# Attention values from weight tiles of 512 rows by 512 columns

## The chip, the cores and the metric

The kernel runs on one core of a Trainium2 chip. What counts is the device time of one execution in microseconds. Five engines work side by side: TensorE (PE in the profile, its weight loads PEld) multiplies matrices and writes to PSUM, VectorE (DVE), ScalarE (ACT) and GpSimd (POOL) do the rest, and SyncE (SP) issues most of the DMAs.

## What is computed

The reference runs 256 tokens of 1024 features through two layers of a first block and then through a second block. The change touches the values of two attentions. In layer 0 of the first block the mixer is a differential attention of four heads beside a pooling branch:

```python
def even_mixer(h, w_in, w_out, ...):
    proj = h @ w_in
    q = proj[..., :A_QK_COLS].reshape(B, S, A_HEADS, 2, A_QK_DIM)
    k = proj[..., A_QK_COLS:2 * A_QK_COLS].reshape(B, S, A_HEADS, 2, A_QK_DIM)
    v = proj[..., 2 * A_QK_COLS:2 * A_QK_COLS + A_WIDTH].reshape(B, S, A_HEADS, A_V_DIM)
...
    o = diff_attention(q[..., 0, :], q[..., 1, :], k[..., 0, :], k[..., 1, :], v, lam, bias_dist)
```

In both layers a cross-attention reads a memory of 256 tokens, the same for both layers:

```python
def cross_attention(h, mem_n, wq, wkv, wo):
    q = (h @ wq).reshape(B, S, X_HEADS, X_HEAD_DIM)
    kv = (mem_n @ wkv).reshape(B, M, 2, X_HEADS, X_HEAD_DIM)
    s = jnp.einsum('bshd,bmhd->bhsm', q, kv[:, :, 0]).astype(jnp.float32) * X_HEAD_DIM ** -0.5
    p = jax.nn.softmax(s, axis=-1)
    o = jnp.einsum('bhsm,bmhd->bshd', p.astype(h.dtype), kv[:, :, 1]).reshape(B, S, D_MODEL)
    return o @ wo
```

The first attention has 512 columns of values (`A_WIDTH`), the memory 1024 in each layer.

## The kernel before

Activations stand with features on partitions. Every operand of a large product is the sum of two float32r parts, `hi` and `lo`; a product is three matmuls, hi by hi, hi by lo and lo by hi. Weights come as tiles of 1 MB, cut on the host (`TILES`, `_tiles`), in one fixed order (`plan`, `self.order`). A tile is loaded by SP into one of four staging buffers (`dma_next`), then split in two halves (`prep_next`): ScalarE casts a half to `hi` (line 319), VectorE subtracts it from the float32 weights to give `lo` (line 198). The two parts lie in a ring of four buffers each, so a tile's first cast waits until TensorE has read the tile four places before it for the last time. `take` hands out the next tile, `pump` keeps three ready.

`pair` makes two blocks of 128 output features from one tile: weights are the stationary operand and 256 tokens stream. For values the tokens have to be on partitions, so `natural` turns this round: blocks of 128 tokens are stationary, the weights stream, 256 columns at a time. A tile of 1024 rows by 256 columns gives 2 blocks of tokens by 8 blocks of rows by 3 matmuls, which is 48. Its result is one bank of PSUM, taken from three that rotate (`gbank`). Scores, turned weights and outputs use four others (`abank`).

The orders of TensorE and of SP are those of the program text. ScalarE, VectorE and POOL are put in order by the framework's planner when the kernel is built: at each engine the first ready instruction by its estimate, those of higher priority first; `high_priority(-later)` lowers the priority of weight casts, of the memory's operand and of some pooling work. A buffer that is named by tag comes free when all that reads it is done; until then the next writer waits.

In the first attention (`layer0_mixer`) the keys, queries and the pooling's inputs come first, then scores of heads 0 and 1, then: values 0, turn of head 0 (`diff_T`), scores 2, output 0 (`diff_out`), turn 1, values 1, output 1, scores 3, then the keys of the memory (`mem_k`). `diff_T` transposes a head's weights on TensorE, and ScalarE copies them to `pt` (line 639), a buffer of tag `sq`. There are two of these, and POOL's window sums (`pool_step`, tiles `pwt`) use them too. `vals` evacuates values to `dv`, part of `dvu`, on ScalarE.

In the cross-attention (`cross`) four value tiles are made by `mem_v`, and the rest of the work is hung between them by the table `after`. `turn` is `x_T`: four transposes and a split of the result into two tiles `xpt`, both of tag `sq`. `out` is `x_out`: 12 matmuls of the values `vh` and `vl` with `xpt`, then a split into the operand of the output product.

Of the kernel before, what the change touches and what calls it, by code (L numbers as in the profile page):

```python
# [30 lines left out]
# columns of the table of parameter vectors, 128 values to a column  # L31
# [9 lines left out]
for _n, _k in VCOLS:  # L41
# [5 lines left out]
# matrices of weights, cut into tiles of k blocks of 128 rows by n columns  # L47
TILES = {
    "ab_w_in": (8, 256), "ab_w_out": (8, 256), "conv_w_in": (8, 256), "conv_w_out": (8, 256),
    "xattn_wq": (8, 256), "xattn_wkv": (8, 256), "xattn_wo": (8, 256), "mlp_w1": (8, 256),  # L50
# [5 lines left out]
def _tiles(a, k, n):  # L56
    """[layers, rows, columns] to [layers, row tile, column tile, partition, k * n]"""
    l, r, c = a.shape
    a = a.reshape(l, r // (k * P), k, P, c // n, n).transpose(0, 1, 4, 3, 2, 5)
    return np.ascontiguousarray(a).reshape(l, r // (k * P), c // n, P, k * n)  # L60


def _layout(inputs):
    """weights by tiles, activations and parameter vectors with features on partitions"""
    out = {}
    for name, (k, n) in TILES.items():
        a = np.asarray(inputs[name])
# [5 lines left out]
    # the modulation's weights with output features on partitions  # L73
# [66 lines left out]
class Operand:  # L140
    """an activation, features on partitions, as the sum of two float32r parts"""
# [16 lines left out]
class Kernel:  # L158
# [53 lines left out]
    def w(self, key, name, l, c0, ncol):  # L212
        """256 columns at a time of a matrix of 1024 rows"""
        for c in range(c0 // T, (c0 + ncol) // T):
            self.order.append((key, self.a[name][l, 0, c], 256, 8))

    def plan(self):
# [4 lines left out]
        w("u", "ab_w_in", 0, 1536, 512), w("v", "ab_w_in", 0, 1024, 512)  # L222
        w("xk", "xattn_wkv", 0, 0, D)
# [9 lines left out]
        w("xk", "xattn_wkv", 1, 0, D)  # L233
# [15 lines left out]
    def plan_ada(self, start, j, span, n=12):  # L249
        """n loads of the modulation's weights among the items from start"""  # L250
# [9 lines left out]
    X_ORDER = tuple((key, i) for key in ("xq", "xv") for i in range(4))  # L260

    def plan_x(self, l):
        for key, h in self.X_ORDER:
            if key == "xq":
                self.w("xq", "xattn_wq", l, T * h, T)
            else:
                self.w("xv", "xattn_wkv", l, D + T * h, T)
        self.w("xo", "xattn_wo", l, 0, D)
# [16 lines left out]
    def dma_next(self, part=None, parts=4):  # L285
        """the next weights from DRAM, all of them or a part"""
# [131 lines left out]
    def norm_mean(self, acc, parts=False):  # L418
        """mean of squares over D, on every partition: PSUM [P, T]"""
# [11 lines left out]
    def rsqrt(self, out, m, scratch, scale=1.0, gain=1.0, eps=EPS):  # L431
        """out = gain * (scale * m + eps) ** -0.5: a guess by exp and ln, and one Newton step"""
# [31 lines left out]
    def norm_columns(self):  # L464
        """1 / 16 of the norm's scale as columns by token: [P, 2]"""
# [7 lines left out]
    def r_columns(self, r, c=None):  # L473
        """r [P, T], the same on every partition, as columns by token: [P, 2]"""
# [11 lines left out]
    def pair(self, key, x, ko=False, bank=None, start=True, stop=True, k0=0, k1=8, w=None,  # L486
             mid=None):
        """two blocks of 128 output features: [P, 2, T]"""
# [12 lines left out]
    def halves(self, key, x, k0):  # L501
        """four pairs: the blocks of x from k0 for all of them first, then the others"""
# [10 lines left out]
    def natural(self, key, x, w=None):  # L513
        """[token, 2, 256 output features] with tokens on partitions"""
        wh, wl = w or self.take(key)
        v = self.gbank().rearrange("p (t n) -> p t n", t=2)
        for t in range(2):
            s = slice(t * P, (t + 1) * P)
            for k in range(8):
                self.mm(v[:, t, :], x.hi(k, s), wh[:, k, :], t == 0 and k == 0, False)  # L520
                self.mm(v[:, t, :], x.lo(k, s), wh[:, k, :], False, False)
                self.mm(v[:, t, :], x.hi(k, s), wl[:, k, :], False, t == 1 and k == 7)
        return v
# [5 lines left out]
    def residual(self, i, v, col, last_norm=None):  # L529
        """h += v for pair i, then the next module's operands"""  # L530
# [36 lines left out]
    def diff_setup(self):  # L567
        """the bias by distance, then its band for every query row; lambda"""
# [110 lines left out]
    def pool_windows(self):  # L679
        """means over windows, less the token itself"""  # L680
# [7 lines left out]
    def pool_step(self, i):  # L688
        """the windows of pair i of the groups"""
# [51 lines left out]
    def layer0_mixer(self):  # L741
# [46 lines left out]
        def vals(i):  # L788
            v = self.natural("v", x)
            for t in range(2):  # L790
                self.actf(self.dv[:, t, 256 * i:256 * i + 256], v[:, t, :], AF.Copy,
                          scale=rc[:, t:t + 1])
            self.pump()

        pts = {}
        vals(0)
        pts[0] = self.diff_T(e.pop(0))
        e[2] = self.diff_scores(2)
        self.diff_out(0, pts.pop(0))
        pts[1] = self.diff_T(e.pop(1))  # L800
        vals(1)
        self.diff_out(1, pts.pop(1))
        e[3] = self.diff_scores(3)
# [38 lines left out]
    def mem_v(self, i, vx):  # L842
        v = self.natural("xv", self.mem)
        self.split(*(a[:, :, 256 * i:256 * i + 256] for a in vx), v)
        self.pump()
# [42 lines left out]
    def cross(self, l):  # L888
# [16 lines left out]
        def out(h):  # L905
# [3 lines left out]
                 ("xv", 1): [(out, 0), (turn, 1), (scores, 3)],  # L909
# [718 lines left out]
```

## Time and profile before

| what | value |
| --- | --- |
| median of 3 runs | 1122.86 us (1122.46 to 1123.25) |
| span of the profiled execution | 1120.5 us |
| mean granted clock of TensorE in it | 0.994 |
| instructions | 21438 |

The profile is of one execution, whose span from the first to the last instruction is 1120.5 us; no other time of that execution is given, and the median of the runs is 2.4 us above it. Times within the trace count from the start of the span. In a row of a timeline a duration is that of one instruction, or from the first to the last of several that stand together; durations of matmuls overlap, so what one costs in a stream is read from start to start. `[4.07 <-ACT pt L639]` says that the engine was idle for 4.07 us and that ScalarE's `pt` of line 639 ended that. L189 is the line in the helper `mm`, L198 that in `tt`, L205 that in `actf`.

### The profile page before, as it was taken

Reading aid. Unit: us, or ns where it says so; the run is one execution under the profiler, and the core shown is the slowest. Engines: PE = TensorE matmul, PEld = TensorE weight load, DVE = VectorE, ACT = ScalarE, POOL = GpSimd, SP = SyncE. Lnnn points to the kernel's source line nnn. Section 1 sums busy time; section 2 is a strip of 40 time slices with the busy share of each in tenths; the row PEclk is TensorE's granted clock in tenths of the full one; section 3 lists DMA queues with packets and bytes.
Section 4 is the critical chain, followed back from the end, with each engine's and each line's share of the span. In section 5 each row is a group of like instructions: output and inputs, shape, how many; then the busy total and the mean of one; then the engine's idle time right before and its main releaser. Section 6 shows DMA issues by size and latency. Waiting matters only on the chain.

```text
span 1120.5 us, 21438 instructions
## 1 busy us (share of the span) xinstructions
PE 1094.8 (98%) x9043; PEld 1084.8 (97%) x9043; DVE 772.2 (69%) x1173; ACT 579.5 (52%) x934; POOL 122.8 (11%) x113
## 2 busy tenths in 40 slices
PE   7789999999999999999999999999999999999998
PEld 6689999999999999999999999999999999999998
DVE  6497666886666686674659877656986679555552
ACT  6465554654444464454546544446766657544441
POOL 4130100200000020110001000003222012111110
PEclk9899999999999999999999999999999999999999
DMA  8845454487666555555428877644543335545521
GB/s 254 234 156 186 147 192 145 164 324 256 251 255 256 220 181 188 188 189 188 151 77 334 320 288 275 256 153 171 189 151 114 113 114 197 217 177 183 178 103 39
DMA packets 32747, 217.75 MB, mean 194 GB/s; under 512 B 3683, under 2 KB 4748, under 8 KB 7308
## 3 DMA queue, kind: packets, MB, share of 16 engines
q1 hardware_dynamic: 32560, 216.34, 54.2%
q8 instruction: 71, 1.16, 0.4%
q14 instruction: 24, 0.20, 0.1%
q10 hardware_dynamic: 92, 0.05, 0.0%
HBM read 214.80 MB, written 1.05 MB: 193 GB/s over the span
## 4 chain that ended last, share of the span: by engine, by line
PE 90%; DVE 4%; DMA 3%; ACT 1%; POOL 1%; issue 1%; SPq 0%; DVEq 0%; ACTq 0%; POOLq 0%
PE g L189 59%; PE a L189 30%; DMA stg<-in_ab_w_in_dram 2%; DVE lo L198 2%; DVE xl L201 1%; POOL pwt L198 1%; ACT hi L319 1%; DMA h<-in_xT_dram 0%; POOL acc L198 0%; ACT sq L205 0%; PE a L873 0%; DVE h L201 0%; DVE h L198 0%; PE a L1220 0%; PE a L1326 0%
## 5 line engine op out<-in xcount | busy, mean ns | idle before, releaser
L198 DVE TENSOR_TENSOR lo<-stg,hi 128x1024 fp32r<-128x1024 f32 (+1 forms) x356 | 437.9, 1246 | 182.3 <-ACT hi L319 179.3
L319 ACT CAST hi<-stg 128x1024 fp32r<-128x1024 f32 (+1 forms) x356 | 361.8, 1039 | 387.4 <-PE g L189 212.8
L189 PE MATMUL g<-xh,hi 128*128 128x256 f32 (+1 forms) x1408 | 402.6, 286 | 7.9 <-ACT hi L319 7.6
L189 PE MATMUL g<-xh,lo 128*128 128x256 f32 (+1 forms) x1408 | 399.3, 284 | 1.5 <-DVE lo L198 1.5
L189 PE MATMUL g<-xl,hi 128*128 128x256 f32 (+1 forms) x1408 | 398.1, 283 | 0.8 <-DVE xl L201 0.8
L189 PEld LDWEIGHTS g<-xh,hi 128*128 128x128 f32 x1408 | 267.3, 190 | 10.9 <-ACT hi L319 9.3
L189 PEld LDWEIGHTS g<-xl,hi 128*128 128x128 f32 x1408 | 268.1, 190 | 2.2 <-DVE xl L201 1.0
L189 PEld LDWEIGHTS g<-xh,lo 128*128 128x128 f32 x1408 | 267.5, 190 | 2.6 <-DVE lo L198 2.6
L189 PE MATMUL a<-uh,lo 128*128 128x256 f32 x800 | 226.4, 283 | 0.0
L189 PE MATMUL a<-uh,hi 128*128 128x256 f32 x800 | 226.3, 283 | 0.0
L189 PE MATMUL a<-ul,hi 128*128 128x256 f32 x800 | 226.3, 283 | 0.0
L189 PEld LDWEIGHTS a<-uh,lo 128*128 128x128 f32 x800 | 152.7, 191 | 0.0
L189 PEld LDWEIGHTS a<-ul,hi 128*128 128x128 f32 x800 | 152.6, 191 | 0.0
L189 PEld LDWEIGHTS a<-uh,hi 128*128 128x128 f32 x800 | 152.6, 191 | 0.0
L189 PE MATMUL g<-uh,hi 128*128 128x256 f32 x288 | 81.7, 284 | 0.0
L189 PE MATMUL g<-ul,hi 128*128 128x256 f32 x288 | 81.5, 283 | 0.0
L189 PE MATMUL g<-uh,lo 128*128 128x256 f32 x288 | 81.5, 283 | 0.0
L198 POOL TENSOR_TENSOR acc<-sq 128x256 f32<-128x256 f32 x10 | 7.9, 791 | 545.0 <-ACT sq L205 369.0
L1066 DVE CUSTOM_DVE_ANT_0 stg<-stg,crow 128x1024 f32<-128x1024 f32 x48 | 57.5, 1220 | 5.6 <-DMA stg<-in_w_ada_dram 5.4
L189 PEld LDWEIGHTS g<-uh,lo 128*128 128x128 f32 x288 | 55.2, 192 | 0.0
L189 PEld LDWEIGHTS g<-ul,hi 128*128 128x128 f32 x288 | 55.2, 192 | 0.0
L189 PEld LDWEIGHTS g<-uh,hi 128*128 128x128 f32 x288 | 55.2, 192 | 0.0
(300 smaller groups left out, 1369.7 us busy)
## 6 DMA issues: line engine op xcount, KB each, us to landing
stg<-in_mlp_w_dram SPq DMA_DIRECT2D x64, 1024.0 KB, 5.0
stg<-in_w_ada_dram SPq DMA_DIRECT2D x24, 1024.0 KB, 5.2
stg<-in_xattn_wkv_dram SPq DMA_DIRECT2D x16, 1024.0 KB, 4.8
stg<-in_w_in_dram SPq DMA_DIRECT2D x16, 1024.0 KB, 4.8
stg<-in_w_mlp_in_dram SPq DMA_DIRECT2D x16, 1024.0 KB, 4.8
stg<-in_w_mlp_out_dram SPq DMA_DIRECT2D x16, 1024.0 KB, 4.8
stg<-in_conv_w_in_dram SPq DMA_DIRECT2D x12, 1024.0 KB, 4.9
stg<-in_xattn_wq_dram SPq DMA_DIRECT2D x8, 1024.0 KB, 4.9
```

The lines of the kernel that those rows point to most:

```text
L189: self.nc.tensor.matmul(out, lhsT, rhs, start=start, stop=stop, skip_group_check=True)
L198: (eng or self.nc.vector).tensor_tensor(out=out, in0=a, in1=b, op=op)
L201: (eng or self.nc.vector).scalar_tensor_tensor(out=out, in0=a, scalar=s, in1=b, op0=op0, op1=op1)
L319: self.nc.scalar.copy(hi[:, s], t[:, s])
L1066: self.nc.vector.tensor_tensor_reduce(out=t[:, b, :], in0=t[:, b, :], in1=self.c_row, op0=ALU.mult, op1=ALU.add, scale=1.0, scalar=0.0, ac ...
```

## The change

Values are made from tiles of 512 rows by 512 columns, and 512 columns stream per matmul. A pair of tiles, upper and lower rows, gives both token blocks, each in a bank of its own, which stay open through both tiles. One tile now has 2 blocks of tokens by 4 blocks of rows by 3 matmuls, 24, and the last of the three reads the high part of the weights (before it was the low part). Values are evacuated once per pair of tiles and token block. The matrices are cut apart on the host so that values have their own arrays; loads stay 1 MB each.

The work between the tiles is put in another order. In the first attention outputs 0 and turn 1 now follow the second tile, since no value is complete before. In the cross-attention output 0 moves behind the third tile, and turn 3 ahead of output 2.

```diff
 TILES = {
...
+    "ab_w_v": (4, 512), "xattn_wq": (8, 256), "xattn_wk": (8, 256), "xattn_wv": (4, 512), "xattn_wo": (8, 256), "mlp_w1": (8, 256),
...
+    parts = {"ab_w_v": ("ab_w_in", 1024, 1536), "xattn_wk": ("xattn_wkv", 0, D),
+             "xattn_wv": ("xattn_wkv", D, 2 * D)}
...
+    def w_wide(self, key, name, l, c0=0):
+
+        for r in range(2):
+            self.order.append((key, self.a[name][l, r, c0 // 512], 512, 4))
...
-        w("u", "ab_w_in", 0, 1536, 512), w("v", "ab_w_in", 0, 1024, 512)
-        w("xk", "xattn_wkv", 0, 0, D)
+        w("u", "ab_w_in", 0, 1024, 512), self.w_wide("v", "ab_w_v", 0)
+        w("xk", "xattn_wk", 0, 0, D)
...
     def plan_x(self, l):
...
+        self.w("xq", "xattn_wq", l, 0, D)
+        for c in range(2):
+            self.w_wide("xv", "xattn_wv", l, 512 * c)
         self.w("xo", "xattn_wo", l, 0, D)
...
-    def natural(self, key, x, w=None):
...
-        wh, wl = w or self.take(key)
-        v = self.gbank().rearrange("p (t n) -> p t n", t=2)
+    def natural(self, key, x, banks=None):
+
+
+        wh, wl = self.take(key)
+        k0 = 4 if banks else 0
+        banks = banks or [self.gbank() for _ in range(2)]
         for t in range(2):
             s = slice(t * P, (t + 1) * P)
-            for k in range(8):
-                self.mm(v[:, t, :], x.hi(k, s), wh[:, k, :], t == 0 and k == 0, False)
-                self.mm(v[:, t, :], x.lo(k, s), wh[:, k, :], False, False)
-                self.mm(v[:, t, :], x.hi(k, s), wl[:, k, :], False, t == 1 and k == 7)
-        return v
+            for k in range(4):
+                self.mm(banks[t], x.hi(k0 + k, s), wh[:, k, :], k0 + k == 0, False)
+                self.mm(banks[t], x.hi(k0 + k, s), wl[:, k, :], False, False)
+                self.mm(banks[t], x.lo(k0 + k, s), wh[:, k, :], False, k0 + k == 7)
+        return banks
...
         pts = {}
-        vals(0)
+        banks = self.natural("v", x)
+        self.pump()
         pts[0] = self.diff_T(e.pop(0))
         e[2] = self.diff_scores(2)
+        self.natural("v", x, banks)
+        for t in range(2):
+            self.actf(self.dv[:, t, :], banks[t], AF.Copy, scale=rc[:, t:t + 1])
+        self.pump()
+        pts[1] = self.diff_T(e.pop(1))
         self.diff_out(0, pts.pop(0))
-        pts[1] = self.diff_T(e.pop(1))
-        vals(1)
+        e[3] = self.diff_scores(3)
         self.diff_out(1, pts.pop(1))
-        e[3] = self.diff_scores(3)
...
     def mem_v(self, i, vx):
-        v = self.natural("xv", self.mem)
-        self.split(*(a[:, :, 256 * i:256 * i + 256] for a in vx), v)
+        self.vbanks = self.natural("xv", self.mem, self.vbanks if i % 2 else None)
+        if i % 2:
+            for t in range(2):
+                s = slice(256 * (i - 1), 256 * (i + 1))
+                self.split(vx[0][:, t, s], vx[1][:, t, s], self.vbanks[t])
         self.pump()
...
         after = {("xv", 0): [(turn, 0), (scores, 2)],
-                 ("xv", 1): [(out, 0), (turn, 1), (scores, 3)],
-                 ("xv", 2): [(out, 1), (turn, 2)], ("xv", 3): [(out, 2), (turn, 3)]}
+                 ("xv", 1): [(turn, 1), (scores, 3)],
+                 ("xv", 2): [(out, 0), (out, 1), (turn, 2)], ("xv", 3): [(turn, 3), (out, 2)]}
```

## Rows read from the trace of the kernel before

**Rows 1.** Page, part 1: busy time, share of the span, instructions of each engine.
```profile
PE 1094.8 (98%) x9043; PEld 1084.8 (97%) x9043; DVE 772.2 (69%) x1173; ACT 579.5 (52%) x934; POOL 122.8 (11%) x113
```

**Rows 2.** Waits of TensorE: us in total, times, longest.
```profile
...
PE a L189 <- ACT pt L639: 4.1, 1, 4.1
...
```

**Rows 3.** Timeline of TensorE, first attention: start us, us, work, idle before.
```profile
58.70 0.47 PE L189 MATMUL g<-hi,xh 128*128 128x256 f32 x1
...
64.58 0.27 PE L635 MATMUL a<-small,de 128*128 128x128 f32 x1
...
65.00 0.93 PE L189 MATMUL a<-dqk 64*128 64x256 f32 x8
70.00 1.65 PE L189 MATMUL a<-dvu,pt 128*128 128x128 f32 x6 [4.07 <-ACT pt L639]
...
79.74 0.39 PE L189 MATMUL g<-memh,hi 128*128 128x256 f32 x1
```

**Rows 4.** Stretches: length, busy us (instructions) of each engine, granted clock, DMA.
```profile
69.50:72.90 3.40, 2.90 (x13) 2.90 (x14) 3.40 (x14) 2.37 (x7) 0.87 (x1) 0.50 0.58 243
135.00:138.50 3.50, 2.42 (x19) 2.09 (x18) 3.50 (x7) 1.69 (x4) 0.00 (x0) 1.00 0.52 143
```

**Rows 5.** Timeline of POOL, first attention.
```profile
67.79 1.65 POOL L198 TENSOR_TENSOR pwt<-pwt 128x269 f32<-128x269 f32 x2
```

**Rows 6.** Timeline of ScalarE, first attention.
```profile
69.47 0.48 ACT L639 COPY pt<-a 128x384 f32<-128x384 f32 x1 [3.03 <-POOL pwt L198]
...
73.97 0.19 ACT L205 ACTIVATION_READ_ACCUMULATOR de<-de,dnm 128x1 f32 x1
...
74.67 2.19 ACT L526 CAST memh<-memr 128x512 fp32r<-128x512 f32 x4
...
79.15 0.83 ACT L205 ACTIVATE dvu<-g,rc 128x256 f32<-128x256 f32 x2
```

**Rows 7.** Timeline of TensorE, first value tile of the first cross-attention.
```profile
158.38 0.28 PE L189 MATMUL g<-hi,memh 128*128 128x256 f32 x1
...
164.15 0.60 PE L873 MATMUL a<-small,xe 128*128 128x128 f32 x4
```

**Rows 8.** The only products of 512 columns: by shape, then one pair's timeline.
```profile
L189 PE MATMUL a<-hsq,small 128*128 128x512 f32 x8 | 4.1, 592 | 0.0
...
800.60 1.02 PE L189 MATMUL a<-hsq,small 128*128 128x512 f32 x2
```

**Rows 9.** Timeline of VectorE, first attention.
```profile
70.59 0.41 DVE L613 CUSTOM_DVE_ANT_0 de<-a,bias 128x256 f32<-128x256 f32 x1
...
72.10 0.15 DVE L617 TENSOR_SCALAR dnm<-dmx 128x4 f32<-128x4 f32 x1
```

**Rows 10.** Timeline of TensorE, end of the third value tile, cross-attention.
```profile
180.63 0.28 PE L189 MATMUL g<-lo,memh 128*128 128x256 f32 x1
...
182.17 0.60 PE L873 MATMUL a<-small,xe 128*128 128x128 f32 x4
182.53 0.36 PE L189 MATMUL g<-hi,memh 128*128 128x256 f32 x1
```

**Rows 11.** Timeline of ScalarE, the same place.
```profile
180.82 1.05 ACT L319 CAST hi<-stg 128x1024 fp32r<-128x1024 f32 x1 [1.64 <-PE g L189]
...
183.68 0.60 ACT L526 CAST xpt<-a 128x512 fp32r<-128x512 f32 x1
```

**Rows 12.** Timeline of VectorE, the same place.
```profile
181.91 1.23 DVE L198 TENSOR_TENSOR lo<-stg,hi 128x1024 fp32r<-128x1024 f32 x1 [1.87 <-ACT hi L319]
183.05 0.68 DVE L198 TENSOR_TENSOR vl<-g,vh 128x512 fp32r<-128x512 f32 x1
...
185.38 0.68 DVE L198 TENSOR_TENSOR xpt<-a,xpt 128x512 fp32r<-128x512 f32 x1
```

**Rows 13.** Timeline of VectorE, during the first value tile.
```profile
159.87 0.68 DVE L198 TENSOR_TENSOR xqt<-g,xqt 128x512 fp32r<-128x512 f32 x1
```

More of the change, by code (lines that the diff above doesn't have):

```diff
@@ L49 @@
     "ab_w_in": (8, 256), "ab_w_out": (8, 256), "conv_w_in": (8, 256), "conv_w_out": (8, 256),
-    "xattn_wq": (8, 256), "xattn_wkv": (8, 256), "xattn_wo": (8, 256), "mlp_w1": (8, 256),
+    "ab_w_v": (4, 512), "xattn_wq": (8, 256), "xattn_wk": (8, 256), "xattn_wv": (4, 512), "xattn_wo": (8, 256), "mlp_w1": (8, 256),
     "mlp_w2": (4, 512), "w_in_2": (8, 256), "w_out_2": (8, 256),
@@ L65, in _layout @@
     out = {}
+    parts = {"ab_w_v": ("ab_w_in", 1024, 1536), "xattn_wk": ("xattn_wkv", 0, D),
+             "xattn_wv": ("xattn_wkv", D, 2 * D)}
     for name, (k, n) in TILES.items():
-        a = np.asarray(inputs[name])
+        of, c0, c1 = parts.get(name, (name, 0, None))
+        a = np.asarray(inputs[of])[:, :, c0:c1]
+        if name == "ab_w_in":
+            a = np.concatenate([a[:, :, :1024], a[:, :, 1536:]], axis=2)
         if name == "w_in_2":
@@ L232, in plan @@
         w("co", "conv_w_out", 0, 0, D)
-        w("xk", "xattn_wkv", 1, 0, D)
+        w("xk", "xattn_wk", 1, 0, D)
         self.plan_x(1)
@@ L258, in plan_ada @@
                 k += 1
-    X_ORDER = tuple((key, i) for key in ("xq", "xv") for i in range(4))
     def plan_x(self, l):
[L263 to L267, printed above, removed]
+        self.w("xq", "xattn_wq", l, 0, D)
+        for c in range(2):
+            self.w_wide("xv", "xattn_wv", l, 512 * c)
         self.w("xo", "xattn_wo", l, 0, D)
@@ L786, in layer0_mixer @@
         self.do = do.rearrange("p a b -> p (a b)").rearrange("p (t h d) -> p t h d", t=2, h=4)
[L788 to L793, printed above, removed]
         pts = {}
-        vals(0)
+        banks = self.natural("v", x)
+        self.pump()
         pts[0] = self.diff_T(e.pop(0))
         e[2] = self.diff_scores(2)
+        self.natural("v", x, banks)
[3 more added lines that the diff above has]
+        pts[1] = self.diff_T(e.pop(1))
         self.diff_out(0, pts.pop(0))
-        pts[1] = self.diff_T(e.pop(1))
-        vals(1)
+        e[3] = self.diff_scores(3)
         self.diff_out(1, pts.pop(1))
-        e[3] = self.diff_scores(3)
         self.new_k()
```

## The prediction

> **What bounds the kernel now.** I read the page first: TensorE is busy 98% of 1120.5 us and its weight loads 97%; no other engine is above 69% [rows 1]. So time is TensorE's stream of products plus what it waits. The list of its waits is next: there are few, and one of them, 4.1 us on ScalarE's copy `pt`, lies right between the two tiles that the change touches [rows 2]. The time of the median, 1122.86 us, is 2.4 us above the span of the profiled execution; I work in the span and add 2.4 at the end. 0.2%, what this kernel can be told from no change by, is 2.25 us.
>
> In the first attention the reader is to see [rows 3]: value tile one from 58.70, the transposes of turn 0 at 64.58, scores 2 from 65.00 for 0.93, nothing until 70.00, then `diff_out(0)`, turn 1, value tile two, and the first keys of the memory at 79.74. The clock fell during the wait: 0.50 from 69.5 to 72.9 [rows 4]; the 2.90 us of work in that stretch ran at half rate, which cost somewhat under half of it, about 1.3 us. The wait's cause is not TensorE's: `pt` takes a buffer of tag `sq`, which POOL's window sums still use. They end at 67.79 + 1.65 = 69.44 [rows 5], and the copy starts at 69.47 [rows 6]. In the cross-attention TensorE now waits for nothing between its value tiles.
>
> **The products.** A value tile of 48 products ran from 158.38 to 164.15 [rows 7]: 0.120 us each, start to start. The tile becomes 24 products of 512 columns. No float32r product that wide is in the trace. Upper bound: twice 0.120 = 0.240, no gain. Lower bound: two plain float32 products of 512 columns at 800.60 take 1.02 us together and 0.592 alone, so they start 0.43 apart [rows 8], nearly twice the 0.240 that 512 float32r columns cost now. My estimate from this is that plain float32 passes twice over its columns, and a pass is 0.214; it can hardly be less for float32r. I take 0.218, near the lower end: every product still has its own weight load (9043 loads for 9043 products [rows 1]), but half as many loads stand beside the same columns. Gain per old pair: 0.240 - 0.218 = 0.022; ten tiles hold 240 pairs: 5.3 us, of which 1.1 in the first attention and 2.1 in each cross-attention.
>
> The Trainium skill, "TensorE: Matmul & The Clock Gate", section "Back-to-back issue gap", gives columns / 2.4 + 2.5 ns for products alone: by it two of 256 cost 218 ns and one of 512 costs 216, and the change would gain 0.6 us instead of 5.3. The trace has 0.120 for one of 256, not 0.109 [rows 7], so the row speaks for the larger gain.
>
> **What is moved in the first attention.** `diff_out(0)` and the second turn now come after both value tiles. The 4.1 us wait goes: tile two fills it. But `dv` is evacuated after tile two alone, in two copies that stand in ScalarE's order behind the exponentials of scores 2, since those are ready first by dependence. VectorE gives their maxima late: it starts on the reduction at 70.59 and has the negated maxima at 72.10 [rows 9], so the exponentials go on to 73.97 + 0.19; memory casts follow at 74.67 [rows 6]. In the new order tile one ends at 63.9 (24 x 0.218 = 5.2), turn and scores take 1.2, tile two ends at 70.4 and the second turn at 70.8, where TensorE comes to `diff_out(0)`. The exponentials end at 74.16; the two copies, an estimated 0.5 each (half the columns took 0.83 for two [rows 6]), end at 75.2 with nothing between them and at 76.8 with three memory casts of 0.53 between (four took 2.19 [rows 6]). So a new wait of 4.4 to 6.0 us; I take 5.4, as two casts are likely ready by then. All of TensorE stands behind it. What was covered before is then late: the first copies of `dv` had the whole 4.1 us for themselves. The clock falls again, 1.3 us. Sum here: -1.1 - 4.1 - 1.3 + 5.4 + 1.3 = +0.2. With the copies ahead of the exponentials the wait would be 1 us; next late is the memory operand, whose casts end at 74.67 + 2.19 [rows 6], so `xk` could not start before about 76, 2 us after TensorE is there. That floor gives -1.1 - 4.1 - 1.3 + 1 + 2 = -3.5.
>
> **What is moved in the cross-attention.** `turn(1)` now stands before `out(0)`. The two parts of a turned `xpt` take both buffers of tag `sq`, so the copy of turn 1 can't start before `out(0)` has read turn 0's, and `out(1)` follows `out(0)` at once on TensorE. Its operand is late by a whole evacuation. Counted from the start of the third tile's last product (180.63 before [rows 10]): ScalarE begins the next weight tile's first cast 0.35 later, as it does now at 180.82 after the last read of the high part [rows 11], and the second 0.95 after that (the pitch of casts), free at 2.26. `out(0)` ends at 1.8, too late to come before the second cast. The `xpt` cast, 0.60 [rows 11], ends at 2.86. VectorE: the first subtraction begins at 1.39 and holds it 1.14 (181.91 to 183.05 [rows 12]), the second is ready then and holds it to 3.67; `xpt`'s own, 0.68 [rows 12], ends at 4.35. `out(1)` would have had its second product at 1.74 and gets it at 4.4: a wait of 2.7 us. Without the second cast and subtraction in the way it is 1.5. Behind it stand turn 2, the fourth tile and all that follows.
>
> `out(2)` needs the fourth tile's values at once. The order within a tile changes too: the high part is now read by the last product, so the cast of the next weights no longer gets ahead of the values' evacuation (at 180.82 it did, by one product [rows 10, 11]). The values' cast (0.58) and subtraction (0.68) then end 1.7 after the last product starts; four transposes take 0.36 [rows 10] and five products 0.6, so the sixth waits 0.5. If the cast comes first it is 2.0. I take 0.5.
>
> Per cross-attention: -2.1 + 2.7 + 0.5 = +1.1; two: +2.2. The clock: it fell to 0.50 in the 4.1 us wait, and stayed at 1.00 around 136, where TensorE worked 2.42 of 3.5 us [rows 4]. A wait of 2.7 with one product in it lies between; I count one fall in two, +1.3.
>
> **At no cost.** The number and size of weight loads stay, and their casts; SP's order of DMAs is the same 1 MB steps. Two of three PSUM banks are held through two tiles: the second bank is first written 12 products (2.6 us) after 158.38, and its last reader, the subtraction at 159.87 [rows 13], ends at 160.55: covered by 0.4 us, else it costs what it is late. Fewer, wider copies of `dv` save ScalarE some 0.2 us that nobody waits for.
>
> **Sum.** +0.2 + 2.2 + 1.3 = +3.7 us: span 1124.2, time 1126.6.
>
> **Rivals.** (a) Faster: the copy of turn 1 is not held up (another buffer, or the engines are free sooner). Then each cross-attention gives -2.1 + 0.5, and with +0.2 the sum is -3.0: 1119.9. For it: VectorE sits idle for 1.87 us just before that place now [rows 12]. It decides where `out(1)` waits under 0.4 us. Against: the two tiles of `xpt` and the two buffers are in the code. Chance 0.16. (b) The wait of the first attention shrinks to the floor of -3.5 while the cross waits come as forecast: -3.5 + 2.2 = -1.3, 1121.6, same. For it: the order on ScalarE is the planner's, and no row shows it. Chance 0.18. (c) The change does not do what it says: a product of 512 columns costs 0.240. Then 5.3 comes on top: 1131.9. Against it is the pass of 0.214 [rows 8]. Chance 0.06. (d) In a stream of loads and products the load sets the pace, and a wide product costs hardly more than a narrow one, 0.120: then the gain is 240 x 0.120 = 28.8 in place of 5.3, and the time 1103.1. For it: loads are as busy as products [rows 1]. Against it, the pass of 0.214. Chance 0.03. The Trainium skill, same page and section, states 131 ns for 512 columns in a sustained stream, by which it would be 1105.7; no row here shows such a rate.
>
> **How the numbers follow.** My forecast, waits in both cross-attentions and a wait exchanged for a wait in the first attention, has 0.57. Its own range: without a fall of the clock in a cross-attention 1125.3, with the first wait at 4.4 us 1124.3 besides; with two falls, 2.0 at `out(2)` and 6.0 in the first attention 1131.5. Case (a) reaches down to 1119.9, (b) to 1121.6. The range 1120.3 to 1131.3 leaves out (c), (d) and half of (a). Faster (below 1120.6): 0.13 of (a), (d) and a little of (b), 0.18. Same (to 1125.1): most of (b), the rest of (a) and a seventh of the forecast, 0.27. Slower: 0.55.
>
> **What would show it.** Right: products of 512 columns 0.215 to 0.220 apart; no wait on POOL's buffers at 66; in its place TensorE waiting for `dv` near 71 to 76; in both cross-attentions a wait of `out(1)` for `xpt` of about 2.7 us, the first product on ScalarE's cast and the second on VectorE's subtraction; half a microsecond before `out(2)`. The forecast is wrong if `dv` is copied before the exponentials, or if the second cast waits behind `xpt`.

## The result

The changed kernel takes 1132.26 us (median of 4 runs, 1129.50 to 1133.01) beside 1122.71 us for the kernel before: a ratio of 1.0079, 95% interval 1.0065 to 1.0094. It is slower, as forecast, but by 9.5 us where 3.7 were forecast, and it lies outside the range that was given (1120.3 to 1131.3). The span of the profiled execution is 1130.0 us, 9.5 more than before. In its lines matmuls are of line 195 (189 before), `pt` of 648 (639), casts of weights of 326 (319), other splits of 535 and 204 (526 and 198), evacuations of 211 (205).

The page, part 1, of the kernel after; it answers to [rows 1]:

```profile
PE 1098.7 (97%) x8803; PEld 1075.9 (95%) x8803; DVE 771.7 (68%) x1173; ACT 579.5 (51%) x932; POOL 122.7 (11%) x113
```

240 products fewer, and yet TensorE is busy 3.9 us longer. Its waits (us in total, times, longest) answer to [rows 2]:

```profile
...
PE a L195 <- ACT dvu L211: 4.5, 2, 3.1
PE a L195 <- DVE xpt L204: 2.4, 2, 1.2
PE a L195 <- ACT xpt L535: 2.3, 2, 1.2
...
PE a L195 <- DVE vl L204: 0.4, 2, 0.2
...
```

The 4.1 us for `pt` are gone. In their place stand a wait for `dvu` in the first attention and, once in each cross-attention, waits for the two halves of `xpt` and for `vl`. The timeline of TensorE in the first attention, against [rows 3]:

```profile
64.45 0.27 PE L644 MATMUL a<-small,de 128*128 128x128 f32 x1
...
71.61 0.27 PE L646 MATMUL a<-small,de 128*128 128x128 f32 x1
75.00 0.71 PE L195 MATMUL a<-dvu,pt 128*128 128x128 f32 x4 [3.12 <-ACT dvu L211]
77.13 0.80 PE L195 MATMUL a<-dvu,pt 128*128 128x128 f32 x2 [1.42 <-ACT dvu L211]
...
80.75 0.56 PE L195 MATMUL g<-memh,hi 128*128 128x256 f32 x1
...
87.97 0.36 PE L195 MATMUL g<-memh,hi 128*128 128x256 f32 x1
```

Output 0 waits twice, once for each copy of `dv`. ScalarE shows why; against [rows 6]:

```profile
74.19 0.18 ACT L211 ACTIVATION_READ_ACCUMULATOR de<-de,dnm 128x1 f32 x1
74.28 0.66 ACT L211 ACTIVATE dvu<-g,rc 128x512 f32<-128x512 f32 x1
74.85 1.64 ACT L535 CAST memh<-memr 128x512 fp32r<-128x512 f32 x3
76.40 0.68 ACT L211 ACTIVATE dvu<-g,rc 128x512 f32<-128x512 f32 x1
```

The first copy stands behind the exponentials, which end with the first line, the second behind three casts of the memory. The last line of TensorE above is the second tile of the memory's keys. It began at 85.78 before and begins at 87.97 now, with the first value tile at 58.70 in both: this stage lost 2.2 us. The stretches around these places in which the granted clock was low, 0.50 or the lower of its two levels, 1.2 GHz in place of 2.4 (length, busy us and instructions of each engine, clock, DMA), against [rows 4]:

```profile
76.60:83.40 6.80, 6.27 (x28) 5.66 (x29) 5.75 (x17) 4.94 (x17) 0.00 (x0) 0.50 0.00 0
185.80:189.30 3.50, 3.50 (x17) 3.31 (x16) 0.93 (x3) 1.17 (x2) 0.10 (x1) 0.51 0.76 281
```

The second one is in the first cross-attention, at output 1. Three timelines of that place, against [rows 10 to 12]. TensorE:

```profile
183.74 0.38 PE L195 MATMUL a<-xpt,vh 128*128 128x256 f32 x1 [1.15 <-ACT xpt L535]
185.31 0.39 PE L195 MATMUL a<-xpt,vh 128*128 128x256 f32 x1 [1.19 <-DVE xpt L204]
```

ScalarE:

```profile
181.21 1.99 ACT L326 CAST hi<-stg 128x1024 fp32r<-128x1024 f32 x2 [1.51 <-PE g L195]
183.11 0.57 ACT L535 CAST xpt<-a 128x512 fp32r<-128x512 f32 x1
```

VectorE:

```profile
182.30 2.36 DVE L204 TENSOR_TENSOR lo<-stg,hi 128x1024 fp32r<-128x1024 f32 x2 [1.74 <-ACT hi L326]
184.57 0.68 DVE L204 TENSOR_TENSOR xpt<-a,xpt 128x512 fp32r<-128x512 f32 x1
```

The cast and the subtraction of `xpt` each come right behind both halves of the next weight tile. From the first value tile to the first product of `xo`, the output product, the first cross-attention took 158.38 to 190.07 before and takes 160.56 to 196.81 now, 4.6 us more; the second 538.68 to 570.37 and 545.29 to 579.97, 3.0 more. With the 2.2 of the first attention this makes 9.8, where the span has grown by 9.5.

Last, a value tile of the first cross-attention, start to start; against [rows 7]:

```profile
160.56 0.39 PE L195 MATMUL g<-hi,memh 128*128 128x512 f32 x1
160.79 0.39 PE L195 MATMUL g<-lo,memh 128*128 128x512 f32 x1
161.02 0.39 PE L195 MATMUL g<-hi,meml 128*128 128x512 f32 x1
...
166.13 0.60 PE L882 MATMUL a<-small,xe 128*128 128x128 f32 x4
```

24 products from 160.56 to 166.13: 0.232 each, not 0.218. A tile takes 5.57 us; it took 5.77.

### The profile page after: what moved, and what is told of

Same layout as the page of the kernel before. It is cut to its first block, busy times and chain, and to the rows that moved or that the text cites. A ratio compares the mean times of both kernels' runs of the same rounds, so it can differ in the third digit from the quotient of the medians.

```text
span 1130.0 us, 20958 instructions
## 1 busy us (share of the span) xinstructions
PE 1098.7 (97%) x8803; PEld 1075.9 (95%) x8803; DVE 771.7 (68%) x1173; ACT 579.5 (51%) x932; POOL 122.7 (11%) x113
## 3 DMA queue, kind: packets, MB, share of 16 engines
HBM read 214.80 MB, written 1.05 MB: 191 GB/s over the span
## 4 chain that ended last, share of the span: by engine, by line
PE 88%; DVE 5%; DMA 2%; ACT 2%; POOL 1%; issue 1%; DVEq 0%; SPq 0%; ACTq 0%; POOLq 0%
PE g L195 58%; PE a L195 30%; DVE lo L204 3%; DMA stg<-in_ab_w_in_dram 2%; ACT hi L326 1%; DVE xl L207 1%; POOL acc L204 1%; ACT sq L211 0%; DMA h<-in_xT_dram 0%; ACT de L211 0%; ACT xh L211 0%; PE a L882 0%; DVE h L207 0%; DVE h L204 0%; DVE de L622 0%
```

## The experiments

**Own buffers.** The kernel after, with odd heads' `xpt` in another tag, and scores 3 ahead of turn 1:

```diff
-    def x_T(self, e):
+    def x_T(self, e, tag="sq"):
...
-        pt = [self.sm.tile([P, 2, T], F32R, tag="sq", name=self.nm("xpt")) for _ in range(2)]
+        pt = [self.sm.tile([P, 2, T], F32R, tag=tag, name=self.nm("xpt")) for _ in range(2)]
...
-            pts[h] = self.x_T(es.pop(h))
+            pts[h] = self.x_T(es.pop(h), "tb" if h % 2 else "sq")
...
-                 ("xv", 1): [(turn, 1), (scores, 3)],
+                 ("xv", 1): [(scores, 3), (turn, 1)],
```

> The changed kernel, with the turned weights of heads 1 and 3 in two buffers of another tag (tb) and turn 1 behind scores 3, where those buffers are free. Theory (turn 1's copy waits for the two buffers of tag sq, which out(0) still reads): the waits before out(1), 1.15 + 1.19 us in each cross-attention beside the product between them, go in both, 5.5 us together, and with them the fall of the clock in the first one, about 1.5 us. The time is about 7 us below that of the changed kernel, near 1125. Rival (the copy is late because ScalarE and VectorE stand behind the split of the next weight tile, whatever the buffers): the waits stay above 1.5 us each and the time within 2 us of the changed kernel.

Measured: 1124.57 us (10 runs), ratio 1.0016 [1.0006, 1.0025]. The waits for `xpt` are gone from both cross-attentions, and so is the low stretch of the clock there; that in the first attention stays, from 77.0 for 6.8 us. From the kernel after 7.7 us are won back with the product width as it is. The second tile of keys begins at 88.23, 2.45 later than before, and up to the last cross-attention the distance stays between 2.4 and 2.6: in this run the cross-attentions cost 0.1 us each over before, and what is left of the loss arises in the first attention (2.19 us; 0.26 stood already at the first value tile, at 58.96). The run changes the buffers and the place of turn 1 together and does not tell their shares apart; what it takes away is that turn 1's copy waits for output 0. The waits of this run:

```profile
PE a L195 <- ACT dvu L211: 4.3, 2, 2.9
...
PE a L195 <- DVE vl L204: 0.5, 2, 0.2
```

**256 columns again.** The kernel after with each product of 512 columns made as two of 256; order and tiles stay:

```diff
-                self.mm(banks[t], x.hi(k0 + k, s), wh[:, k, :], k0 + k == 0, False)
...
+                for c in (slice(0, 256), slice(256, 512)):
+                    o = banks[t][:, c]
+                    self.mm(o, x.hi(k0 + k, s), wh[:, k, c], k0 + k == 0 and c.start == 0, False)
...
```

> The changed kernel, with each product of 512 columns made as two of 256, and nothing else. Theory (a product of 512 columns costs 0.232, two of 256 cost 0.239): the ten value tiles take 240 x 0.007 = 1.8 us more in all; 1.5 to 2.5 us above the changed kernel. Rival (the width is worth the forecast 0.022 per product and was lost in waits elsewhere): 5 us or more above it.

Measured: 1132.21 us, ratio 1.0087 [1.0070, 1.0104]: the time of the kernel after. So it is not 1.5 to 2.5 us above that kernel, as the theory had it, nor the rival's 5. But a value tile takes 5.76 us from its start to the next work, 0.19 more than with 512 columns, so the ten tiles cost 1.9 more, which is what the theory has for the tiles. The time hides this because the clock was low for 3.4 us in the first attention in place of 6.8, with the second keys at 86.68; in the cross-attentions it fell once, as after, though in the second of them.

**The order alone.** The kernel before, narrow, with nothing new but the table of the cross-attention:

```diff
-                 ("xv", 1): [(out, 0), (turn, 1), (scores, 3)],
-                 ("xv", 2): [(out, 1), (turn, 2)], ("xv", 3): [(out, 2), (turn, 3)]}
+                 ("xv", 1): [(turn, 1), (scores, 3)],
+                 ("xv", 2): [(out, 0), (out, 1), (turn, 2)], ("xv", 3): [(turn, 3), (out, 2)]}
```

> The kernel before, with 256 columns and narrow tiles, and only the new table of what stands between the value tiles of the cross-attention. Theory (the order makes the wait): out(1) waits for xpt in both cross-attentions, longer than in the changed kernel, since the third tile's own values are evacuated in between too: about 3.3 us each, no wait at out(2). 6 to 9 us above the kernel before, with or without a fall of the clock. Rival (the wait comes from values that arrive in pairs of tiles): no wait, and the time of the kernel before within 1 us.

Measured: 1133.24 us, ratio 1.0095 [1.0080, 1.0110]. The order alone makes a loss as large as that of the whole change, 10.4 us where 6 to 9 were expected. Each cross-attention takes 36.6 us from its first value tile to `xo`, 4.9 more than before. Its waits:

```profile
PE a L189 <- ACT xpt L526: 3.0, 2, 1.5
PE a L189 <- DVE xpt L198: 2.6, 2, 1.3
```

Its low stretches of the clock:

```profile
69.00:75.80 6.80, 6.09 (x28) 6.09 (x29) 6.80 (x27) 5.59 (x18) 1.02 (x2) 0.50 0.31 129
185.10:188.50 3.40, 3.20 (x16) 3.20 (x16) 0.74 (x2) 0.45 (x1) 0.00 (x0) 0.50 0.80 279
570.80:574.20 3.40, 3.19 (x15) 3.19 (x16) 0.75 (x2) 0.44 (x1) 0.00 (x0) 0.50 0.81 284
```

In the first attention this kernel has the order of the kernel before, and the same wait of 4.1 us for `pt`, ending at 69.7; but the clock stayed low for 6.8 us, where in [rows 4] it was 3.4. The second keys begin at 86.93, 1.15 later, though the first value tile began 0.35 earlier, at 58.35.

**Scores 2 behind the second tile.** The kernel after, with one line of the first attention moved:

```diff
         pts[0] = self.diff_T(e.pop(0))
-        e[2] = self.diff_scores(2)
         self.natural("v", x, banks)
         for t in range(2):
             self.actf(self.dv[:, t, :], banks[t], AF.Copy, scale=rc[:, t:t + 1])
         self.pump()
+        e[2] = self.diff_scores(2)
```

> The changed kernel, with scores 2 of the first attention behind the second value tile and its evacuation. Theory (the copies of dv are late because they stand behind the exponentials of scores 2 on ScalarE, and these wait for VectorE): the wait for dv of 5.3 us (71.9 to 77.1) shrinks to 2 to 3, held by the memory's casts that stand before the second copy, and the clock doesn't stay low for 6.8 us: 3 to 6 us below the changed kernel. Rival (the wait is the evacuation after the second tile itself): the wait stays above 4 us and the time within 1.5 us.

Measured: 1132.1 us, ratio 1.0084 [1.0069, 1.0099]: no gain. The stage did as the theory says: the wait for `dv` fell from 4.5 to 2.4 us (a new one of 0.6 for `dmx`, VectorE's maxima, stands behind it), and the stage from first value tile to second keys from 29.27 to 27.10 us. The profiled execution has this back in two other places: value tile one, which lies ahead of the edit, began 1.3 later (59.99), and the second cross-attention, in which the clock now fell too, took 1.6 more:

```profile
570.30:573.70 3.40, 3.40 (x14) 2.92 (x13) 1.38 (x2) 1.17 (x2) 0.00 (x0) 0.50 0.64 267
```

**Wide products in the cross-attentions only.** The run with own buffers, with tiles, products and order of the first attention from the kernel before:

```diff
-    "ab_w_v": (4, 512), ...
+    "ab_w_v": (8, 256), ...
...
-                 self.w_wide("v", "ab_w_v", 0)
+                 w("v", "ab_w_v", 0, 0, 512)
...
```

> Wide products in the cross-attentions only, with the buffers and the order of the run with own buffers; the first attention is that of the kernel before. In the run with own buffers all the loss lay in the first attention (second tile of keys at 88.23 against 85.78, then the same distance of about 2.4 up to the end), so theory: the same as the kernel before, 1122.8 (1122.3 to 1123.5), each cross-attention ending within 0.2 us of before, since 96 products by 0.014 saved is 0.7 us in the tiles and the wait of output 2 takes 0.7. Rival, products of 512 columns worth 0.022 per old pair: 1119 or so.

Measured: 1123.6 us beside 1123.07 (11 and 27 runs), ratio 1.0001 [0.9992, 1.0010]. The first cross-attention takes 33.24 us from the last scores ahead of its values to `xo`, where the kernel before takes 33.11. So the wide products with their waits taken away are worth nothing: what the tiles give, output 2 takes, because it now needs the values of the tile just finished.

**No wait at output 2 either.** The same, with `pt` in a tag of its own and output 1 between turn 3 and output 2:

```diff
-                 ("xv", 2): [(out, 0), (out, 1), (turn, 2)], ("xv", 3): [(turn, 3), (out, 2)]}
+                 ("xv", 2): [(out, 0), (turn, 2)], ("xv", 3): [(turn, 3), (out, 1), (out, 2)]}
```

> The one with wide crosses, with pt in a buffer of another tag, and output 1 moved from behind the third value tile to between turn 3 and output 2, where its 1.3 us lie over the 0.7 us that output 2 waits for values. Theory: 2.7 less by pt, 0.7 less in each cross-attention: 1118.7 (1118 to 1120). Rival, the clock falls at another place or the copies of turn 3 are late by output 1: 1120 to 1121.

Measured: 1123.5 us, ratio 1.0004 [0.9995, 1.0013], neither the 1118.7 of the theory nor the rival's 1120 to 1121. In the first cross-attention `xo` now begins 0.66 us earlier (32.58 us after the last scores in place of 33.24). Of this 0.58 went again at once, in a wait of `xo`, 13 products on, for the operand that output 1 now gives later:

```profile
193.87 0.39 PE L195 MATMUL g<-ul,hi 128*128 128x256 f32 x1 [0.42 <-DVE ul L204]
```

The 2.7 us by `pt` did not come either; the run with `pt` in a buffer of its own, below, shows why.

**The width by itself.** The run with own buffers, with value products of 384 columns in the first cross-attention and 128 in the second:

```diff
+            n = 512 if key == "v" else 128 if self.cross_l else 384
             for k in range(4):
+                m = 512 if k0 + k == 0 else n
-                self.mm(banks[t], x.hi(k0 + k, s), wh[:, k, :], k0 + k == 0, False)
+                self.mm(banks[t][:, :m], x.hi(k0 + k, s), wh[:, k, :m], k0 + k == 0, False)
...
```

> The run with own buffers again, with value products cut to 384 columns in the first cross-attention and to 128 in the second (the rest of the columns is left out but for the first row block, so the output is not the full sum). If a product is a fixed part and a part per column, the two prices 0.120 and 0.232 give 0.44 ns per column and 0.008 fixed: 0.176 us for 384 and 0.064 for 128. If the weight load sets a floor, 128 columns stay near 0.1 or above. If only widths above 256 are dearer, 384 lies above 0.18.

Measured: 1109.66 us in one run, which leaves out part of the products; what counts here is the timeline of TensorE at both places, where the granted clock was 1.00:

```profile
160.63 0.33 PE L195 MATMUL g<-hi,memh 128*128 128x384 f32 x1
...
161.68 0.34 PE L195 MATMUL g<-hi,memh 128*128 128x384 f32 x1
...
541.54 0.27 PE L195 MATMUL g<-lo,memh 128*128 128x128 f32 x1
...
543.88 0.28 PE L195 MATMUL g<-lo,memh 128*128 128x128 f32 x1
```

384 columns: 6 intervals in 1.05 us, 0.175 each. 128 columns: 21 intervals in 2.34, 0.111 each. From 256 columns up the price is nearly a straight line, 0.12, 0.175, 0.232: 0.44 ns a column and 0.008 us fixed. Below, it is nearly flat: two halves of a 256 would cost 0.222. The theory holds for 384 (0.176 expected) and falls for 128 (0.064 expected): there the rival, a floor, is right. The Trainium skill, "TensorE: Matmul & The Clock Gate", section "LDWEIGHTS (loading the stationary operand)", gives columns / 1.2 ns for a load, by which one of 128 columns takes an estimated 107 ns. The 0.111 agrees with a load for each product setting the pace; that it is the load is not shown, since no run here has such products without a load of their own. By the Trainium skill, same page, section "Back-to-back issue gap", a sustained stream has 81 ns at 128 columns and 131 at 512. Here the trace has 111 and 232, and the measurement decides.

**`pt` in a buffer of its own.** The kernel before with one edit:

```diff
-        pt = self.sm.tile([P, 384], F32, tag="sq", name=self.nm("pt"))
+        pt = self.sm.tile([P, 384], F32, tag="ad", name=self.nm("pt"), bufs=3)
```

> The kernel before with one edit: pt takes a buffer of another tag, which POOL's window sums do not use. If the 4.1 us wait in the first attention is POOL's buffer, TensorE goes on some 3 us earlier there and the clock does not fall; the memory's operand, whose casts ended at 74.67 + 2.19 and whose subtractions follow, is then late, so the first keys of the memory start near 77 instead of 79.74, and the second near 83 instead of 85.78. Time about 1120 (1119.5 to 1121). The rival, that something else on ScalarE or TensorE makes the wait: the same as before, 1122.8.

Measured: 1123.9 us, ratio 1.0005 [0.9996, 1.0014], not the 1120 that was expected. The timeline of TensorE says why; the last line is the start of the second value tile:

```profile
67.27 0.94 PE L189 MATMUL a<-dvu,pt 128*128 128x128 f32 x6 [0.93 <-ACT pt L639]
71.36 0.48 PE L635 MATMUL a<-small,de 128*128 128x128 f32 x1 [3.16 <-DVE dmx L613]
...
71.91 0.56 PE L189 MATMUL g<-hi,xh 128*128 128x256 f32 x1
```

In the kernel before the same tile starts here:

```profile
71.94 0.56 PE L189 MATMUL g<-hi,xh 128*128 128x256 f32 x1
```

The wait for POOL's buffer is gone: 4.07 became 0.93, so that was its cause. Right behind it turn 1 waits 3.16 us for VectorE's maxima of scores 2, and the second value tile starts when it did before. The clock stayed low for 6.8 us, from 70.3.

**Turn 1 behind the second tile.** The last kernel, with `vals(1)` ahead of `pts[1] = self.diff_T(e.pop(1))`; and the same with the wide cross-attentions.

> The kernel before with pt in its own tag, as in the run with that edit alone, and turn 1 moved behind the second value tile. That run showed a second wait of 3.3 us right behind the one taken away: turn 1 wants a bank of PSUM that VectorE still reads for scores 2. If that is all, the second value tile now runs from 68 to 73.7 at the full clock, output 1 follows near 75, and the first keys of the memory start near 77, when their operand is ready; the second keys near 83 instead of 85.78. Time 1120.3 (1119.5 to 1121.5). Rival: the stage is bound by a chain through VectorE and ScalarE whatever TensorE does first, then a third wait comes in its place and the time stays at 1122.5 to 1124.

> The same first attention (narrow tiles, own pt, turn 1 behind the second tile) with wide products in both cross-attentions, in the order and with the buffers that left no long wait. In the run with wide cross-attentions alone these were worth nothing (0.1 us each way), so theory: the same time as the run without them, 1120.3. Rival, 0.7 us of gain in each cross-attention: 1119.

Measured: 1125.47 us, ratio 1.0019 [1.0011, 1.0028], and 1125.01, 1.0017 [1.0008, 1.0026]. The rival has the cause right, a third wait comes in its place; the times are above even its 1122.5 to 1124.

```profile
73.23 0.27 PE L637 MATMUL a<-small,de 128*128 128x128 f32 x1
78.79 1.43 PE L189 MATMUL a<-dvu,pt 128*128 128x128 f32 x5 [5.29 <-ACT pt L639]
```

Turn 1's last transpose ended at 73.50; its copy on ScalarE began at 78.27, behind exponentials, casts of the memory, a cast of weights and two copies of `dv`.

**A quarter of the memory's operand.** Two kernels, the run with own buffers and the one with turn 1 behind, in which only pair 0 of the memory is formed and stands for all four; the products stay.

```diff
-            for i in range(4):
+            for i in range(1):
                 v = self.memory_pair(i)
...
```

> The run with own buffers, with only the first quarter of the memory's operand formed (scaled, cast and subtracted) and used four times over, so three casts leave ScalarE and six scalings and three subtractions leave VectorE; all products stay. If the casts of the memory between the two copies of dv set the end of the wait for dv, the second copy comes 1.6 us earlier (74.8 instead of 76.4) and output 0 with it, so the second keys start near 86.6 instead of 88.23, and earlier still if the clock then stays low for less. The rival, that the exponentials set it: the first copy and output 0 where they were, second keys at 88.2.

> The run with turn 1 behind the second value tile, with the same three quarters of the memory's operand left out. There pt of turn 1 was ready at 73.1 and copied at 78.03, behind four exponentials, four casts of the memory, a cast of weights and two copies of dv on ScalarE. If ScalarE's queue is the bound, the wait of 5.3 us before output 1 falls by the three casts, 1.6 us, to 3.7, and the second keys start near 86.5 instead of 88.11. If the memory's operand itself is what the keys wait for, the wait of output 1 falls but the keys move more, by the subtractions on VectorE as well: 85 or earlier.

Measured: 1121.91 and 1124.56 us, one run each. With own buffers both copies of `dv` now follow each other at once, from 74.56 to 75.80, where the run they are taken from has 74.33 and, behind three casts, 76.44; and output 0 runs through:

```profile
75.27 0.95 PE L203 MATMUL a<-dvu,pt 128*128 128x128 f32 x5 [3.17 <-ACT dvu L219]
```

The second keys begin at 85.39, 2.84 earlier: 1.1 by the wait (4.3 to 3.2), where 1.6 was expected, and the rest is what a clock that was low for 3.4 us in place of 6.8 gives back. So the exponentials set the first copy and the casts the second. In the other kernel the wait at output 1 fell from 5.29 to 3.09, more than the 1.6 expected, but the clock stayed low for 6.8 us in place of 3.4; the second keys began at 87.98 (88.11), the stage from the first value tile being 0.9 shorter.

The first attention in the profiled execution of each run, in us (low: length of the low stretch there; stage: from the first value tile to the second keys):

| kernel | waits of outputs and turns there | low | second keys begin | stage |
| --- | --- | --- | --- | --- |
| before | 4.1 (`pt`) | 3.4 | 85.78 | 27.08 |
| after | 3.1 + 1.4 (`dv`) | 6.8 | 87.97 | 29.27 |
| own buffers | 4.3 (`dv`) | 6.8 | 88.23 | 29.27 |
| 256 columns again | 3.9 (`dv`) | 3.4 | 86.68 | 27.39 |
| order alone | 4.1 (`pt`) | 6.8 | 86.93 | 28.58 |
| scores 2 behind | 2.4 (`dv`) + 0.6 (`dmx`) | 3.4 | 87.09 | 27.10 |
| wide cross-attentions only | 3.3 (`pt`) + 0.3 (`dmx`) | 3.4 | 85.56 | 27.03 |
| no wait at output 2 | 0.9 (`pt`) + 3.1 (`dmx`) | 6.8 | 87.99 | 28.58 |
| `pt` on its own | 0.9 (`pt`) + 3.2 (`dmx`) | 6.8 | 87.68 | 28.58 |
| turn 1 behind | 0.9 + 5.3 (`pt`) | 3.4 | 88.11 | 29.70 |
| turn 1 behind, wide cross-attentions | 0.9 + 3.9 (`pt`) | 3.4 | 87.77 | 28.18 |
| own buffers, quarter of the memory | 3.2 (`dv`) | 3.4 | 85.39 | 26.47 |
| turn 1 behind, quarter of the memory | 0.9 + 3.1 (`pt`) | 6.8 | 87.98 | 28.84 |

Before, order alone and wide cross-attentions only have the same order of work on TensorE in this stage; so have `pt` on its own and no wait at output 2.

## Why the prediction was right in direction and wrong in size

**The step that failed: the price of a product of 512 columns.** The prediction took 0.218, by way of a pass of 0.214 ("it can hardly be less for float32r"). The pass was half of the plain float32 product of [rows 8], an estimate, and nothing showed that float32r streams at its rate; 0.218 was taken near that lower end. Measured are 0.232, which is near the upper one, twice 0.120. The straight line from 256 to 512 columns accounts for it. [rows 7] exceed half a pass by 0.013, and the forecast left 0.004 of excess on the wide product; but only 0.008 of it is a fixed part, which a pair of products spares once, and the rest grows with the columns, so 0.018 are left at 512. A tile, with the step to the next work, took 5.57 us where 24 x 0.218 = 5.23 were counted: 0.34 on each of ten tiles, 3.4 of the 5.8 us that the sum missed. In its place the gain of the ten tiles is 10 x 0.20 = 2.0 us, not 5.3. Rival (c), no gain at all (1131.9), was held unlikely on the same ground; the measured 0.232 is closer to its 0.240 than to 0.218.

**A second term too small in the profiled execution: the clock.** The fall in the first attention was counted as 1.3 us both ways, 3.4 us at half rate. After, the clock was low for 6.8 us, in which TensorE worked 6.27: an estimated 3.1 lost, 1.8 more than counted. The one fall counted for the cross-attentions came, in the first of them, and cost 1.7 rather than 1.3, since TensorE worked all through it. With 0.4 for output 2 (below) these terms make 3.4 + 1.8 + 0.4 + 0.4 = 6.0, where 5.8 were missed. The clock's part belongs to that execution: of the four, the one with the highest mean granted clock (0.993, the others 0.990 and 0.991) took 1129.50, inside the range. Nor is the 2.4 added to the span a constant: in every execution with both on record the time is 1.7 to 1.9 above its own span, so the profiled execution of the kernel before was likely one of the quicker ones.

**The first attention: the mechanism right, the size in part by luck.** The wait for POOL's buffer went, and the run with `pt` on its own shows that POOL's buffer was its cause. The forecast put both copies of `dv` behind the exponentials, from 74.2, with casts of the memory between them, ending at 75.2 to 76.8; they ran at 74.28 and 76.40 and ended at 77.08. Counted as the forecast did, from where TensorE comes to output 0 to the end of the copies, the wait was 71.72 to 77.08, the 5.4 us that were forecast (4.5 of it stand as idle time above, since four products ran in between). That it fits is luck: TensorE came 0.9 later than the 70.8 counted, for the dearer products, and the copies ended 0.9 later than the 76.2 that 5.4 stands for, with three casts between them and not two. The run with a quarter of the memory shows that it is those casts that part the copies. Scores 2 behind shows the exponentials' part: with them moved, the wait fell to 2.4 us.

**The cross-attentions: right, but for output 2.** Forecast were 2.7 us at output 1, its first product on ScalarE's cast and the second on VectorE's subtraction, behind both halves of the next tile's weights. Measured are 1.15 + 1.19 of idle time by that release and 2.8 from start to start (183.74 less 182.43, then 185.31 less 183.86). The run with own buffers takes the cause away and the waits go, 7.7 us with the fall of the clock and what follows it; the run with the order alone brings them into the kernel before. That the cast of weights would no longer get ahead of the values came too; output 2 lost 0.7 rather than 0.5 (12 products and the step behind them from 194.67 to 196.81, 2.14, where 1.42 is usual). The values' cast, the weights' casts behind it, and output 2's wait, in the kernel after:

```profile
194.51 0.59 ACT L535 CAST vh<-g 128x512 fp32r<-128x512 f32 x1 [2.21 <-PE g L195]
194.99 2.00 ACT L326 CAST hi<-stg 128x1024 fp32r<-128x1024 f32 x2
...
195.88 0.39 PE L195 MATMUL a<-xpt,vl 128*128 128x256 f32 x1 [0.22 <-DVE vl L204]
```

**The rivals.** (a), a turn that is not held up, would have given 1119.9; the run with own buffers comes closest to that case, and took 1124.57, since the product price, and in its profile the longer low clock in the first attention, hold there too. (b), copies of `dv` ahead of the exponentials, did not come; the quarter of the memory's operand is not that case. Its sum left out the 1.3 us that the forecast counts for the clock in the cross-attentions; with them it would have been 1122.9, still the time of before. (d), a wide product at 0.120, is refuted by 0.232. The idea of (b), that the first attention has some 3 us to give, was tried in three more orders. None brought the stage below the 27.08 us of before: scores 2 behind has 27.10, which only takes back what the change had lost; in `pt` on its own (28.58) and turn 1 behind (29.70) the next wait in the chain through VectorE and ScalarE took the place of the one removed, and in the first of these the clock was also low for longer.

**What stays open.** Why the clock stayed low for 3.4 us in some of these runs and for 6.8 in others. The run with the order alone has the very order of before in the first attention, and a wait that is as long, and yet 6.8, with a stage 1.5 us longer. The length is not the kernel's alone: in 61 executions of the kernel before, beside these runs, the mean granted clock lies between 0.992 and 0.995; the nine at 0.992 take 1123.8 us on average, the 27 at 0.994 take 1122.7. And ahead of the first attention, where the two kernels do not differ in a line, the clock was low for 10.2 us in the kernel before (38.8 to 49.0) and for 6.9 in the run with turn 1 behind (41.2 to 48.1). So of a difference of 1 to 2 us between single profiles, as between the stages in the table, no run here tells how much is the order's and how much the clock's. The loss as a whole is larger than that: the execution of the changed kernel at 0.993 took 1129.5, those of the kernel before at 0.993 take 1123.3 on average. No version that forms the whole output beat the kernel before.

## What to carry to other kernels

A wider product saves only what is fixed in a narrow one: find out from two widths of the same type whether there is a fixed part, and do not take the rate of another type. An order in which two readers of a two-buffer tag stand one behind the other costs a whole evacuation, and that evacuation queues behind whatever its engines took up meanwhile: here 2.8 us. Before a wait is removed, follow the chain to the next wait behind it, and put a price on the clock for every wait that is left. Before a difference of 1 to 2 us between two profiles is explained, see by how much executions of one kernel differ.

## What the runs showed of the hardware that was not expected

A float32r product with its own weight load costs 0.111 us at 128 columns, 0.12 at 256, 0.175 at 384 and 0.232 at 512, at a granted clock of 1.00, while a plain float32 product of 512 columns takes 0.43 [rows 8]. After waits of 2 to 5 us in all that look alike the granted clock was 0.50 for 3.4 us in some runs and 6.8 in others, also where the order of work in that stage is the same (before and order alone). In the cross-attentions, behind the same wait at output 1, the clock fell in the first alone (after), in the second alone (256 columns again) or in both (scores 2 behind).
